# A hybrid decoder kernel: norm steps between the stages emitted one split's length earlier

## The chip, the core and the metric

The kernel runs on one core of a Trainium2 chip. The core has five engines with a queue of instructions each: TensorE (PE) multiplies, VectorE (DVE) and ScalarE (ACT) work elementwise, GpSimd (POOL) does small steps, and SyncE (SP) issues the DMAs. Engines wait for each other by semaphores. The metric is the device time of one execution in microseconds; less is better.

## The reference

Two layers, each a token mixer and a feed-forward network (FFN), both wrapped in RMS norms before and after. All inputs and weights are float32; 256 tokens of width 1024.

```
def rmsnorm(x, g):
    y = xf * lax.rsqrt(jnp.mean(xf * xf, axis=-1, keepdims=True) + RMS_EPS)
    return (y * g.astype(F32)).astype(x.dtype)

def swiglu(h, w_gate, w_up, w_down):
    return (jax.nn.silu(h @ w_gate) * (h @ w_up)) @ w_down

for l in range(DEPTH):
    m = hybrid_mixer(rmsnorm(h, mix_pre_norm[l]), w_in[l], ..., w_out[l])
    h = h + rmsnorm(m, mix_post_norm[l])
    f = swiglu(rmsnorm(h, ffn_pre_norm[l]), w_gate[l], w_up[l], w_down[l])
    h = h + rmsnorm(f, ffn_post_norm[l])
```

The mixer projects to 3088 columns, runs dilated softmax attention (8 heads) beside chunked gated linear attention (4 heads), and projects back with `w_out`. The FFN is 2816 wide.

## The kernel before

The 256 tokens are two row halves of 128, `j` = 0 and 1; each keeps its residual `h[j]` in SBUF. A product must be nearly float32-exact, so each operand is split in two parts of a narrower type: a high part (`wh`, `xh`), which ACT makes by a copy, and a low part (`wl`, `xl`), which DVE makes as operand minus high part. A product is then three matmuls: high by high, low by high, high by low. Weights stream in through four `raw` slots of 128x1024 and are split into eight pairs `wh`/`wl`. One such piece is called a part here: the gate matrix of an FFN chunk (`FF_CHUNKS`) has four parts, the up matrix too, and each serves both row halves. A slot takes its next load when the low half of what was in it has been made.

The FFN's chunks 1, 3 and 4 (`SEVEN`) save one of eight block products by sums of weight blocks (`b11`, `b21`, `v1`, ..., shown as `b` and `v`) and sums of activation blocks (`sums_x`: four `a` sums, split to `sums_h` and `sums_l`).

The order on every engine comes from a planner that runs while the kernel is built (`Clock`). It holds an estimated time for each engine and counts TensorE's as "now". Each piece of work is a generator: `yield t` puts it to sleep until the planner's clock reaches `t`, and then it emits its next instructions. `soon(x)` is the time at which the planner thinks `x` is written. `highs()` and `lows_()` emit the weight splits on ACT and DVE whenever the planner's clock for that engine is no more than `AHEAD` (0.3 and 0.7 us) ahead of now; `loader` emits the loads and `project` the matmuls.

Between the mixer and the FFN, `post_norm` takes the two PSUM banks of `w_out`'s product (`wo`): `square` on ACT (`sq`, `msh`), the gain on DVE (`pn`), `var` on DVE, `rstd` on POOL, and the update of `h` on DVE. `pre_norm_ffn` follows: `sq` on `h`, `var`, `rstd`, the scaled copies `xn` on ACT, TensorE's transposes (`tp_x`), a copy with the gain into `a` (four instructions), `xh_x` on ACT and `xl_x` on DVE; after the second row half come the `a` sums. The FFN of a layer begins with the products `b11` (`seven_a`) and `b21` (`seven_b`) for row half 0, then gate and up of chunk 0 for row half 0, then both for row half 1. ACT loads the table for SiLU in front of its first use, on `p` (the sum of the first two products).

Of the kernel before, what the change touches and what calls it, by code (L numbers as in the profile page):

```python
# [51 lines left out]
UNITS1 = [("gqk", 0), ("aq", 0), ("gqk", 1), ("aq", 1)] + UNITS0[2:]  # L52
BANKS = {"mm": 2, "tp": 2, "ac": 4}
SEM = 0.2


class Engine:
# [50 lines left out]
class Clock:  # L108
# [40 lines left out]
    def note(self, eng, cost, ins, outs):  # L149
# [3 lines left out]
        for ap in ins:  # L153
            r = self.ready(ap)
            start = max(start, r if eng == "PE" and ap in outs else r + SEM)
        if eng == "DMA":
# [21 lines left out]
    def tile(self, pool, shape, dtype, tag, bufs, name):  # L178
# [3 lines left out]
        while len(slots) >= bufs:  # L182
            done = [t for t in slots if t not in self.open]
            if done:
                t = min(done, key=lambda t: self.last.get(t, 0.0))
                slots.remove(t)
                free = self.last.get(t, 0.0) + SEM
                yield free
# [8 lines left out]
    def close(self, *tiles):  # L197
        for t in tiles:
            self.open.discard(t.tensor.name)

    def after(self, new, old):

        self.free[new.tensor.name] = self.last.get(old.tensor.name, 0.0) + SEM

# [33 lines left out]
def trunk(ctx: ExitStack, tc: tile.TileContext, io: dict):  # L238
# [7 lines left out]
    ck = Clock(nc)  # L246
    pe, act, dve, pool, dma, close = ck.pe, ck.act, ck.dve, ck.pool, ck.dma, ck.close

    def at(*aps):
        return ck.ready(*aps) + 0.5  # L250

    def soon(*aps):

        return ck.ready(*aps)

    def bank(tag, name):
        t = yield from ck.tile(ps, [P, 512], F32, tag, BANKS[tag], name)
        ck.port[t.tensor.name] = ("", 0.0)
        return t

    def t2(name):
        return ck.tile(sb, [P, 512], F32, "t2", NT2, name)
# [4 lines left out]
    def small(name, n=1):  # L267
        return sb.tile([P, n], F32, tag="small", bufs=20, name=name)
# [259 lines left out]
    def load_gain(i):  # L528
        if i < len(gains):
            gtiles[i] = gain(gains[i], D, "gain", 1)  # L530


    def rstd_of(parts_, n):

        v = small("var", n)
        if len(parts_) == 1:
            dve.tensor_scalar(v, parts_[0], EPS, None, op0=ALU.add)
        else:
            dve.scalar_tensor_tensor(v, parts_[0], EPS, parts_[1], op0=ALU.add, op1=ALU.add)
        r = small("rstd", n)  # L540
        pool.tensor_tensor(r, v, nhalf[:, :n], op=ALU.pow)
        return r

    def transpose_pe(src, t0, m, tp):
        for i in range(m):
            pe.transpose(tp[:, i * P:(i + 1) * P], src[:, (t0 + i) * P:(t0 + i + 1) * P], ident)
        return tp.rearrange("p (k t) -> p k t", t=P)[:, :m, :]
# [44 lines left out]
    def pre_norm_ffn(j, out, l):  # L592


        ms = []
        for i in range(2):
            c = slice(i * 512, (i + 1) * 512)
            junk = yield from ck.tile(sb, [P, 512], BF16, "t2", NT2, "sq")
            yield soon(h[j][:, c])
            m = small("ms")  # L600
            act.activation(junk, h[j][:, c], AF.Square, scale=1.0 / 32.0, accum_out=m)
            close(junk)
            ms.append(m)
        yield soon(*ms)
        r = rstd_of(ms, 1)
        xs = []
        if j == 0:
            sums_of[l] = []
            for name, dtype in (("a", F32), ("sums_h", R32), ("sums_l", R32)):
                t = yield from ck.tile(sb, [P, 4, 512], dtype, "big", NBIG, name)  # L610
                sums_of[l].append(t)
        while len(sums_of[l]) < 3:
            yield ck.now() + 0.1
        a = sums_of[l][0]
        for i in range(2):
            c = slice(i * 512, (i + 1) * 512)
            x = yield from t2("xn")
            yield soon(r)
            act.activation(x, h[j][:, c], AF.Copy, scale=r)
            xs.append(x)  # L620
        xt = []
        for i in range(2):
            hi = yield from ck.tile(sb, [P, 4, P], R32, f"xt{j}", 6, "xh_x")
            lo = yield from ck.tile(sb, [P, 4, P], R32, f"xt{j}", 6, "xl_x")
            yield at(xs[i])
            tp = yield from bank("tp", "tp_x")
            tv = transpose_pe(xs[i], 0, 4, tp)
            close(xs[i])
            yield soon(tp)
            av = a[:, 2 * j + i, :]  # L630
            for k in range(4):
                g = 16 + 8 * l + 4 * i + k
                act.activation(av[:, k * P:(k + 1) * P], tv[:, k, :], AF.Copy, scale=gcol[:, g:g + 1])
            close(tp)
            yield soon(av)
            act.activation(hi.rearrange("p k t -> p (k t)"), av, AF.Copy)
            yield soon(hi)
            dve.tensor_tensor(lo.rearrange("p k t -> p (k t)"), av,
                              hi.rearrange("p k t -> p (k t)").bitcast(F32), op=ALU.subtract)
            xt += [(hi[:, k, :], lo[:, k, :]) for k in range(4)]  # L640
        out[j] = xt
        if j == 1:
            yield from sums_x(out, l)

    def sums_x(out, l):

        t, hi, lo = sums_of[l]
        yield soon(t)
        dve.tensor_tensor(t[:, 3, :], t[:, 2, :], t[:, 3, :], op=ALU.subtract)
        dve.tensor_tensor(t[:, 2, :], t[:, 0, :], t[:, 2, :], op=ALU.subtract)  # L650
        dve.tensor_tensor(t[:, 0, :], t[:, 3, :], t[:, 0, :], op=ALU.subtract)
        dve.tensor_tensor(t[:, 1, :], t[:, 1, :], t[:, 0, :], op=ALU.add)
        for row, name in ((0, "s2"), (3, "s1"), (2, "s3"), (1, "s4")):
            yield soon(t[:, row, :])
            act.activation(hi[:, row, :], t[:, row, :], AF.Copy)
            yield soon(hi[:, row, :])
            dve.tensor_tensor(lo[:, row, :], t[:, row, :], hi[:, row, :].bitcast(F32),
                              op=ALU.subtract)
            out[2][name] = [(hi[:, row, k * P:(k + 1) * P], lo[:, row, k * P:(k + 1) * P])
                            for k in range(4)]  # L660
        close(t)
        out[2]["tiles"] = (hi, lo)
# [10 lines left out]
    def post_norm(j, banks, gi, then):  # L673

        g = gtiles[gi]
        ms, ts = [], []

        def square(i):
            junk = yield from t2("sq")
            yield soon(banks[i])  # L680
            m = small("msh")
            act.activation(junk, banks[i], AF.Square, scale=1.0 / 32.0, accum_out=m)
            close(junk)
            ms.append(m)

        def gained(i):
            t = yield from t2("pn")
            yield ck.port[banks[i].tensor.name][1]
            dve.tensor_tensor(t, banks[i], g[:, i * 512:(i + 1) * 512], op=ALU.mult)
            close(banks[i])  # L690
            ts.append(t)

        yield from square(0)
        if ck.ready(banks[1]) <= ck.at["Act"]:
            yield from square(1)
            yield from gained(0)
        else:
            yield from gained(0)
            yield from square(1)
        yield soon(*ms)  # L700
        r = rstd_of(ms, 1)
        yield from gained(1)
        yield soon(r)
        for i, w in ((0, 512), (512, 256), (768, 256)) if j and then is None else ((0, 512), (512, 512)):
            c = slice(i, i + w)
            dve.scalar_tensor_tensor(h[j][:, c], ts[i // 512][:, i % 512:i % 512 + w], r, h[j][:, c],
                                     op0=ALU.mult, op1=ALU.add)
            if then is None:
                dma.dma_start(io["out"][0, j * P:(j + 1) * P, c], h[j][:, c])
        close(*ts)  # L710
        if j == 1:
            load_gain(gi + 1)
        if then is not None:
            yield from then


    def mixer(l, xin, xout):
# [482 lines left out]
        for j in range(2):  # L1200
            while mixed[j][4] is None:
                yield ck.now() + 0.2
            bk = []
            for i in range(2):
                o = yield from bank("ac", f"wo{i}")
                bk.append(o)
            for part, lo in (("wo_g", 4), ("wo_a", 0)):
                while mixed[j][lo] is None:
                    yield ck.now() + 0.2
                yield from project((l, part), mixed[j][lo:lo + 4], bk, first=(lo == 4),  # L1210
                                   last=(lo == 0))
                close_x(mixed[j][lo:lo + 4])
            go(post_norm(j, bk, gi, pre_norm_ffn(j, xout, l)))


    def ffn(l, xin, xout):
# [163 lines left out]
        for j in range(2):  # L1380
            yield from down(nch - 2, j)
            yield from down(nch - 1, j)
            then = pre_norm(j, xout, l + 1) if l + 1 < L else None
            ck.spawn(post_norm(j, acc[j], gi, then), ck.now())
# [19 lines left out]
    h = [const.tile([P, D], F32, name=f"h{j}") for j in range(2)]  # L1404
# [110 lines left out]
```

## Time and profile before

| | |
|---|---|
| three runs | 641.35, 641.0, 639.06 us; median 641.0 |
| profiled execution | 639.99 us in all, span 638.2 us |
| TensorE matmul busy | 622.1 us (97%) |
| DVE busy | 504.3 us (79%) |
| ACT busy | 412.6 us (65%) |
| mean granted TensorE clock | 0.989 |
| HBM read | 107.60 MB |

The span runs from the first to the last instruction. Busy time counts instructions that run, not waits; matmuls overlap each other, so a busy TensorE is not TensorE at its peak. In a timeline a row gives start, duration, engine, line, operation, output and inputs, shape and count, and in brackets the idle time before it with what ended it. All instructions bear the line of the recording helper, 77, so they are told apart by names.

### The profile page before, as it was taken

What the parts mean: (1) busy time and instruction counts of PE and PEld (TensorE: products, weight loads), DVE (VectorE), ACT (ScalarE), POOL (GpSimd) and SP (SyncE); (2) the same over time, 40 slices, a digit from 0 to 9 for tenths busy, and PEclk for the clock granted to TensorE, in tenths of its full rate; (3) what the DMA queues carried; (4) which work ended last, traced back from release to release, by engine and by line L of the source; (5) the groups of instructions that cost most, each with busy time, mean ns of one, the idle gap of its engine ahead of it and who ended that gap; (6) DMA issues with size and microseconds to landing.
All of it is one profiled execution on the core that took longest, in us unless ns stands there. A gap on an engine that the chain in (4) does not pass through costs nothing.

```text
span 638.2 us, 10255 instructions
## 1 busy us (share of the span) xinstructions
PE 622.1 (97%) x3896; PEld 510.7 (80%) x3896; DVE 504.3 (79%) x784; ACT 412.6 (65%) x700; POOL 23.7 (4%) x41
## 2 busy tenths in 40 slices
PE   8999999989999999999999999999899999999995
PEld 7987778868888888879788777887788888888894
DVE  4899975579897899987588996557899778989743
ACT  6889855486946385656577797537966555838531
POOL 1000021000000000000010000110000000000000
PEclk9999999979999999999999999999899999999998
DMA  8965455156048946039474714840910895710811
GB/s 281 281 193 156 149 188 191 52 174 255 1 142 294 397 152 201 1 104 289 142 246 149 205 46 126 277 142 17 368 45 3 286 353 216 270 61 1 263 68 66
DMA packets 53108, 109.30 MB, mean 171 GB/s; under 512 B 5890, under 2 KB 10692, under 8 KB 53060
## 3 DMA queue, kind: packets, MB, share of 16 engines
q1 hardware_dynamic: 53060, 108.66, 51.4%
q8 instruction: 30, 0.49, 0.3%
q14 instruction: 18, 0.15, 0.1%
HBM read 107.60 MB, written 1.05 MB: 170 GB/s over the span
## 4 chain that ended last, share of the span: by engine, by line
PE 86%; DVE 5%; DMA 3%; ACT 3%; issue 2%; SPq 1%; POOLq 0%; DVEq 0%; ACTq 0%
PE dn L77 17%; PE seven_a L77 10%; PE gate_ps L77 8%; PE up_ps L77 8%; PE seven_b L77 7%; PE wo L77 4%; PE gr L77 4%; PE gqk L77 4%; PE ak L77 4%; PE gv L77 3%; PE av L77 3%; PE aq L77 3%; DVE wl L77 3%; ACT wh L77 2%; PE att_o L77 2%
## 5 line engine op out<-in xcount | busy, mean ns | idle before, releaser
L77 DVE TENSOR_TENSOR wl<-raw,wh 128x1024 fp32r<-128x1024 f32 (+1 forms) x124 | 150.3, 1221 | 32.4 <-ACT wh L77 31.6
L77 ACT ACTIVATE wh<-raw 128x1024 fp32r<-128x1024 f32 (+1 forms) x124 | 130.0, 1059 | 54.1 <-DMA raw<-w_gate 17.3
L77 ACT ACTIVATE wh<-b 128x1024 fp32r<-128x1024 f32 x72 | 75.0, 1058 | 38.2 <-PE up_ps L77 9.3
L77 DVE TENSOR_TENSOR wl<-b,wh 128x1024 fp32r<-128x1024 f32 x72 | 84.9, 1218 | 2.9 <-ACT wh L77 2.8
L77 PE MATMUL dn<-wh,xh_h 128*128 128x512 f32 x176 | 70.4, 400 | 0.0
L77 PE MATMUL dn<-wl,xh_h 128*128 128x512 f32 x176 | 69.5, 395 | 0.0
L77 PE MATMUL dn<-wh,xl_h 128*128 128x512 f32 x176 | 69.1, 393 | 0.0
L77 DVE TENSOR_TENSOR b<-b,b 128x1024 f32<-128x1024 f32 x36 | 42.7, 1217 | 0.0
L77 POOL TENSOR_TENSOR rstd<-var,nhalf 128x1 f32<-128x1 f32 (+1 forms) x24 | 21.2, 883 | 557.6 <-DVE var L77 557.5
L77 PEld LDWEIGHTS dn<-wl,xh_h 128*128 128x128 f32 x176 | 33.1, 188 | 8.2 <-DVE wl L77 1.4
L77 PEld LDWEIGHTS dn<-wh,xl_h 128*128 128x128 f32 x176 | 33.0, 188 | 7.4
L77 PEld LDWEIGHTS dn<-wh,xh_h 128*128 128x128 f32 x176 | 33.1, 188 | 7.0
L77 DVE SCALAR_TENSOR_TENSOR wl<-raw,gcol,wh 128x512 fp32r<-128x512 f32 (+1 forms) x48 | 34.4, 748 | 1.6 <-ACT wh L77 1.6
L77 ACT ACTIVATE wh<-raw,gcol 128x512 fp32r<-128x512 f32 (+1 forms) x48 | 32.4, 717 | 4.7 <-DMA raw<-w_in 3.3
L77 PE MATMUL gate_ps<-wh,xh_x 128*128 128x512 f32 (+1 forms) x96 | 34.9, 363 | 0.0
L77 PE MATMUL up_ps<-wh,xh_x 128*128 128x512 f32 (+1 forms) x96 | 34.3, 358 | 0.0
L77 PE MATMUL gate_ps<-wh,xl_x 128*128 128x512 f32 (+1 forms) x96 | 34.1, 356 | 0.0
L77 PE MATMUL gate_ps<-wl,xh_x 128*128 128x512 f32 (+1 forms) x96 | 34.1, 355 | 0.0
L77 PE MATMUL up_ps<-wh,xl_x 128*128 128x512 f32 (+1 forms) x96 | 34.1, 355 | 0.0
L77 PE MATMUL up_ps<-wl,xh_x 128*128 128x512 f32 (+1 forms) x96 | 34.1, 355 | 0.0
L77 ACT ACTIVATE xh_h<-tp_h 128x512 fp32r<-128x512 f32 (+1 forms) x24 | 13.3, 554 | 25.1 <-PE tp_h L77 24.9
L77 DVE TENSOR_TENSOR xl_h<-tp_h,xh_h 128x512 fp32r<-128x512 f32 (+1 forms) x24 | 15.5, 645 | 14.9 <-ACT xh_h L77 14.8
(233 smaller groups left out, 1483.9 us busy)
## 6 DMA issues: line engine op xcount, KB each, us to landing
raw<-w_in SPq DMA_DIRECT2D x45, 512.0 KB, 4.6
raw<-w_down SPq DMA_DIRECT2D x44, 512.0 KB, 4.9
b<-w_gate SPq DMA_DIRECT2D x24, 512.0 KB, 8.2
b<-w_up SPq DMA_DIRECT2D x24, 512.0 KB, 7.5
raw<-w_gate SPq DMA_DIRECT2D x20, 512.0 KB, 4.4
raw<-w_up SPq DMA_DIRECT2D x20, 512.0 KB, 4.8
raw<-w_out SPq DMA_DIRECT2D x16, 512.0 KB, 3.7
raw<-w_in SPq DMA_DIRECT2D x6, 256.0 KB, 5.1
```

Source lines behind the costliest of these rows:

```text
L77: return f(*args, **kw)
```

## The change

A constant `LEAD` of 1.1 us and a helper `next_`, which is `soon` less `LEAD`, are added. In `pre_norm_ffn` and `post_norm` the waits of the planner use `next_` in place of `soon`, so these steps are emitted when the planner's clock stands 1.1 us before their inputs; one wait (on `av`) is left out, and one takes `ts` in besides `r`.

```
+LEAD = 1.1
...
+    def next_(*aps):
+
+        return ck.ready(*aps) - LEAD
...
-            yield soon(h[j][:, c])
+            yield next_(h[j][:, c])
             m = small("ms")
             act.activation(junk, h[j][:, c], AF.Square, scale=1.0 / 32.0, accum_out=m)
...
-        yield soon(*ms)
+        yield next_(*ms)
         r = rstd_of(ms, 1)
...
-            yield soon(r)
+            yield next_(r)
             act.activation(x, h[j][:, c], AF.Copy, scale=r)
...
-            yield soon(tp)
+            yield next_(tp)
...
-            yield soon(av)
             act.activation(hi.rearrange("p k t -> p (k t)"), av, AF.Copy)
-            yield soon(hi)
+            yield next_(hi)
...
-            yield soon(banks[i])
+            yield next_(banks[i])
...
-            yield ck.port[banks[i].tensor.name][1]
+            yield ck.port[banks[i].tensor.name][1] - LEAD
...
-        yield soon(*ms)
+        yield next_(*ms)
         r = rstd_of(ms, 1)
         yield from gained(1)
-        yield soon(r)
+        yield next_(r, *ts)
```

The three places below are in layer 0 between the mixer and the FFN; layer 1 has the same order there. `raw_1430`, `raw_1432`, `raw_1451` and `raw_1483` are the four gate parts of chunk 0, `raw_1739` and the next are up parts after the change.

DVE before, around the update of the second row half's `h` (`h1`):

```order
L77 TENSOR_TENSOR wl_1632<-raw_1430,wh_1631 128x1024
L77 TENSOR_TENSOR wl_1647<-raw_1432,wh_1646 128x1024
L77 TENSOR_TENSOR wl_1665<-raw_1451,wh_1664 128x1024
L77 TENSOR_TENSOR pn_1687<-wo0_1561,gain_952 128x512
L77 SCALAR_TENSOR_TENSOR var_1693<-msh_1682,msh_1685 128x1
L77 TENSOR_TENSOR pn_1697<-wo1_1562,gain_952 128x512
L77 TENSOR_TENSOR xl_x_1637<-a_1619,xh_x_1636 128x512
L77 TENSOR_TENSOR wl_1680<-raw_1483,wh_1679 128x1024
L77 SCALAR_TENSOR_TENSOR h1_88<-pn_1687,rstd_1695,h1_88 128x512
```

All four gate parts are split ahead of `h1`. DVE after, from the first gate part on (`h1` stands above, with one split of `b21` and a `var` between):

```order
L78 TENSOR_TENSOR wl_1679<-raw_1430,wh_1678 128x1024
L78 TENSOR_TENSOR wl_1709<-raw_1432,wh_1708 128x1024
L78 TENSOR_TENSOR p1_1715<-seven_b_1717,p1_1715 128x512
L78 TENSOR_TENSOR wl_1738<-raw_1451,wh_1737 128x1024
L78 TENSOR_TENSOR xl_x_1745<-a_1603,xh_x_1744 128x512
L78 TENSOR_TENSOR xl_x_1789<-a_1603,xh_x_1788 128x512
L78 TENSOR_TENSOR a_1603<-a_1603 128x512 x4
L78 TENSOR_TENSOR wl_1765<-raw_1483,wh_1764 128x1024
L78 TENSOR_TENSOR wl_1813<-raw_1739,wh_1812 128x1024
L78 TENSOR_TENSOR sums_l_1605<-a_1603,sums_h_1604 128x512 x4
L78 TENSOR_TENSOR wl_1816<-raw_1753,wh_1815 128x1024
```

All gate parts now come after `h1`; the fourth stands behind both `xl_x` of the second row half and the four `a` sums, and the second up part behind the four `sums_l`.

ACT before, from the third gate part on:

```order
L77 ACTIVATE wh_1664<-raw_1451 128x1024
L77 ACTIVATE sq_1681,msh_1682<-wo0_1561 128x512
L77 ACTIVATE sq_1684,msh_1685<-wo1_1562 128x512
L77 ACTIVATE xh_x_1636<-a_1619 128x512
L77 ACTIVATE wh_1679<-raw_1483 128x1024
L77 ACTIVATE a_1619<-tp_x_1703,gcol_89 128x128 x4
L77 ACTIVATE xh_x_1701<-a_1619 128x512
```

Between the third and the fourth gate part stand two squares and one `xh_x`, the first row half's. ACT after, from the third gate part on:

```order
L78 ACTIVATE wh_1737<-raw_1451 128x1024
L78 ACTIVATE a_1603<-tp_x_1766,gcol_89 128x128 x4
L78 ACTIVATE xh_x_1744<-a_1603 128x512
L78 ACT_TABLE_LOAD
L78 ACTIVATE p1_1715<-p1_1715 128x512
L78 ACTIVATE a_1603<-tp_x_1790,gcol_89 128x128 x4
L78 ACTIVATE xh_x_1788<-a_1603 128x512
L78 ACTIVATE wh_1764<-raw_1483 128x1024
```

The fourth gate part has moved behind the second row half's two sets of copies, the table load and the SiLU.

TensorE's order at this place changes only in where the transposes stand: those of the first row half come after nine and after fifteen of the last 24 matmuls of `wo` (before: after fifteen and after all 24), those of the second one within the gate product for row half 0, behind its first and its second part. In the mixer of layer 1 the order moves on several engines (the transposes of `h`, the `ex` steps of the linear attention, `fine` and `score` products), and SP's loads stay in order but for two small gain loads.

## Rows read from the trace of the kernel before

**Rows 1.** The page: span, and busy time of each engine

```profile
span 638.2 us, 10255 instructions
...
PE 622.1 (97%) x3896; PEld 510.7 (80%) x3896; DVE 504.3 (79%) x784; ACT 412.6 (65%) x700; POOL 23.7 (4%) x41
```

**Rows 2.** Stretches: us, busy PE, PEld, DVE, ACT, POOL, clock, DMA share, GB/s

```profile
133.50:137.00 3.50, 1.10 (x5) 0.37 (x3) 3.02 (x6) 3.50 (x10) 0.55 (x1) 0.89 0.90 290
137.00:143.00 6.00, 5.88 (x14) 4.62 (x15) 4.36 (x6) 4.10 (x11) 0.00 (x0) 0.50 0.88 247
...
329.00:334.00 5.00, 4.66 (x27) 3.64 (x26) 2.71 (x7) 2.49 (x11) 0.00 (x0) 1.00 1.04 403
334.00:430.00 96.00, 95.99 (x926) 78.12 (x925) 72.95 (x187) 65.55 (x143) 4.99 (x8) 1.00 0.51 159
468.00:630.00 162.00, 162.00 (x772) 133.87 (x771) 131.08 (x135) 92.06 (x110) 0.55 (x1) 1.00 0.44 153
```

**Rows 3.** Timeline of TensorE, layer 0, from the seam to the mark

```profile
133.22 0.60 PE L77 MATMUL tp_x<-ident,xn 128*128 128x128 f32 x4
...
135.66 0.50 PE L77 MATMUL seven_a<-wh,xh_x 128*128 128x512 f32 x1 [1.85 <-ACT xh_x L77]
...
137.12 0.80 PE L77 MATMUL seven_a<-wh,xl_x 128*128 128x512 f32 x1 [0.67 <-DVE xl_x L77]
...
151.01 0.39 PE L77 MATMUL up_ps<-wh,xh_x 128*128 128x512 f32 x1
151.24 0.40 PE L77 MATMUL up_ps<-wl,xh_x 128*128 128x512 f32 x1
...
156.99 0.40 PE L77 MATMUL gate_ps<-wh,xh_x 128*128 128x512 f32 x1
```

**Rows 4.** Timeline of TensorE, layer 1, the same two places

```profile
445.32 0.60 PE L77 MATMUL tp_x<-ident,xn 128*128 128x128 f32 x4
...
467.92 0.40 PE L77 MATMUL gate_ps<-wh,xh_x 128*128 128x512 f32 x1
```

**Rows 5.** Timeline of ACT, layer 0, at the seam

```profile
121.27 0.60 ACT L77 ACTIVATE sq<-wo 128x512 f32<-128x512 f32 x1 [2.26 <-PE wo L77]
...
133.83 0.59 ACT L77 ACTIVATE sq<-wo 128x512 f32<-128x512 f32 x1
...
142.29 0.62 ACT L77 ACTIVATE sq<-h 128x512 bf16<-128x512 f32 x1
...
142.90 2.00 ACT L77 ACTIVATE wh<-raw 128x1024 fp32r<-128x1024 f32 x2
...
147.09 1.28 ACT L77 ACT_TABLE_LOAD   x1
148.38 0.63 ACT L77 ACTIVATE p<-p 128x512 f32<-128x512 f32 x1
148.92 1.12 ACT L77 ACTIVATE a<-tp_x,gcol 128x128 f32<-128x128 f32 x4
```

**Rows 6.** Timeline of DVE, layer 0, at the seam

```profile
123.57 1.42 DVE L77 SCALAR_TENSOR_TENSOR h<-pn,rstd,h 128x512 f32<-128x512 f32 x2
...
131.07 2.36 DVE L77 TENSOR_TENSOR wl<-raw,wh 128x1024 fp32r<-128x1024 f32 x2 [0.76 <-ACT wh L77]
...
136.99 1.22 DVE L77 TENSOR_TENSOR wl<-raw,wh 128x1024 fp32r<-128x1024 f32 x1
...
143.03 0.16 DVE L77 SCALAR_TENSOR_TENSOR var<-ms 128x1 f32<-128x1 f32 x1 [1.48 <-ACT sq L77]
...
156.22 2.87 DVE L77 TENSOR_TENSOR a<-a 128x512 f32<-128x512 f32 x4
...
165.87 1.29 DVE L77 TENSOR_TENSOR sums_l<-a,sums_h 128x512 fp32r<-128x512 f32 x2
```

**Rows 7.** Timeline of POOL, layer 0

```profile
127.41 0.55 POOL L77 TENSOR_TENSOR rstd<-var,nhalf 128x1 f32<-128x1 f32 x1 [3.87 <-DVE var L77]
```

**Rows 8.** The page's DMA issues: count, KB each, us from issue to landing

```profile
raw<-w_up SPq DMA_DIRECT2D x20, 512.0 KB, 4.8
```

## The prediction

> **What bounds the kernel now.** I read the page first: the span is 638.2 us and TensorE is busy 97% of it [rows 1]. So a change in order gains only where TensorE waits or runs at its low clock, and it loses wherever it makes TensorE wait. Next I read the table of stretches around the seams between stages [rows 2]. At the seam from the mixer to the FFN in layer 0 (133.5 to 137.0 us) TensorE works 1.10 of 3.50 us. From 137.0 to 143.0 us the granted clock is 0.50, the 1.2 GHz level: 14 matmuls take 5.88 us, 0.42 each. TensorE's timeline [rows 3] names the causes: 1.85 us until ACT has written `xh_x`, then 0.67 us until DVE has written `xl_x`. It idled there, and the clock fell. At full clock matmuls start 0.23 us apart, and a gate or up product of eight steps (24 matmuls) with one block of transposes takes 5.98 us (151.01 to 156.99). In layer 1 the same seam stands 312.10 us later [rows 4]. The seam from the FFN to the next mixer has almost no idle time: 0.34 us in 329 to 334, and 95.99 of 96.00 us are busy up to 430 [rows 2].
>
> I therefore read the time at one mark: the first matmul of the second row half's gate product, at 156.99 in layer 0 and 467.92 in layer 1 [rows 3, 4]. Behind it TensorE is never short of work (162.00 of 162.00 us in layer 1 [rows 2]), so a delay at the mark is a delay of the end.
>
> **The change part by part.** The diff adds no operation. It puts the norm's steps up to 1.1 us earlier into the queues of ACT and DVE, so weight splits fall behind them. A split takes ACT 1.06 us (0.95 until the next starts) and DVE 1.22 us (1.14 until the next) [rows 5, 6]. Each queue runs in the order of emission. I lay out the new order of layer 0 step by step: an instruction starts when its engine is free and its input is written.
>
> First row half: `h` is written from 123.57 as before. The two `sq` steps stand behind one split instead of two, at 124.35 and 125.03. `var` follows its `sq` by 0.74 at least (142.29 to 143.03) [rows 5, 6]; DVE is in a split until 126.05. `var` with its hand-over takes some 0.25 us and `rstd` 0.55 [rows 6, 7], so `xn` starts at 126.9. The transposes stand earlier in TensorE's queue, at 129.3 and 131.05. A block takes 0.60 us, the four scaled copies `a` 1.12, and `xh_x` comes behind them [rows 3, 5]: 131.1 and 132.9, with `xl_x` at 131.8 and 133.5. TensorE is through with `wo` and both blocks at about 133.55 (the last of them started at 133.22 and idleness began at 133.81) and goes on without a pause: **both waits of the seam, 1.85 and 0.67 us, go**.
>
> What is late next? Four splits that were done by 138.2 (the fourth gate part's low half started at 136.99) [rows 6] now stand behind the norm of the second row half.
> - The last split of `b21` reaches ACT at 133.4. The second half's `sq` on `wo` starts at 134.35 (was 133.83), and `h` comes 2.30 us after it, as 121.27 to 123.57 shows [rows 5, 6]: 136.65 to 138.0. Only then DVE splits `b21`: done 139.2. TensorE reaches that part at 137.95: **1.3 us wait**.
> - `sq` on `h` at 137.4 and 138.1, `var` 139.1, `xn` 139.95. The first three gate parts have their low halves at 140.4, 141.55 and 143.5, and TensorE is through with them and both blocks of transposes at 145.4.
> - The fourth gate part has both halves behind the whole path of the second row half. On ACT: `a` 142.4, `xh_x` 143.6, the table load 144.2 (1.28 us), the SiLU on `p` 145.5, `a` 146.05, `xh_x` 147.2, and then the split at 147.7, done 148.8. On DVE: `xl_x` 147.85, the four sums `a` at 148.6, which take 2.87 us, and then the split, 151.4 to 152.6 [rows 5, 6]. TensorE stands from 145.4 to 152.6 but for one matmul: **7.0 us wait**.
> - The up parts: DVE does one split (done 153.75), four `sums_l` (0.61 apart [rows 6]) to 156.1, then three splits, done 157.35, 158.45 and 159.6. The fourth part's load needs the slot that the fourth gate part frees at 152.6 and lands 4.8 us later [rows 8], in time for its place. TensorE ends the gate product at 153.8 and the first up part at 155.2, waits 1.9 us for the second, and is through at 161.3 at full clock.
>
> The clock: waits of 2.5 us in all came before the low level in rows 2 and 3, so I expect it behind the 7 us too, and charge the row's price, 0.42 us a matmul, for as long a stretch as there. The first up part then ends at 157.35, just when the second is ready, so only the tail is dearer: 162.2. I take 161.7, between the row and none. The mark comes 4.7 us later than 156.99 (bounds 4.3 and 5.2). In layer 1 the same steps end at 161.7 + 312.1 = 473.8 against 467.92, 5.9 us later (5.4 and 6.4); before, that seam had lost less.
>
> Behind the mark the sums and splits of the seven products keep a margin: by the same reckoning their low halves are 0.5 to 2.9 us ahead of TensorE, so nothing is added. The mixer of layer 1 is reshuffled too (transposes, `ex`, `fine`, `score`). Its splits run several us ahead, and I take 0, with bounds from the nearest rows: -0.34 (its only idle time goes) and +0.67 (one wait behind a DVE operation, as at 137.12) [rows 2, 3].
>
> On ACT's table load a rule of the Trainium skill speaks against the forecast. The rows [rows 5] show 1.28 us, and the SiLU starts at 148.38, 0.01 us behind it. The page "ScalarE: Activation LUTs", section "What ACT_TABLE_LOAD costs", gives about 2.66 us for a switch, a drain of about 1.38 us being counted beside the load. By the page the two layers would be some 2.8 us dearer, since the load now stands on the path; by the row nothing is added. I go by the row.
>
> **Sum.** 4.7 + 5.9 + 0 = +10.6 us. Span 638.2 + 10.6 = 648.8; the profiled execution took 639.99 in all, so 650.6. The median of the runs, 641.0, lies 1.0 above that execution, and the forecast for a median is 641.0 + 10.6, or **651**. Its own range is 647 to 656: the bounds above, and some 2 us a layer for the rounding of twenty hand-overs between engines.
>
> **The rivals.**
> - **Faster: the seam closes and no split is late.** One mechanism: the fourth gate part's low half is written before TensorE wants it (145.6). Then the mark of layer 0 comes at 133.55 + 24 x 0.23 + 2 x 5.98 = 151.0, 6.0 us earlier, and that of layer 1 4.8 earlier: 641.0 - 10.8 = 630. For it speaks that the waits of the seam do go; against it that DVE's queue has two `xl_x` and four sums in front of that split. The point from which it decides is 148: a split done by then, 4.6 us before my 152.6, offsets the loss. 6 in 100.
> - **Even.** The path of the second row half runs some 4 us quicker than laid out, so that the stall pays back just what the seam gives: 638 to 644. 8 in 100.
> - **Dearer behind the mark.** The margin of 0.5 us at the sums is eaten and DVE falls a split or two (1.14 us each) behind in each layer: 653 to 657. 9 in 100.
> - **The table load holds ACT longer.** It now stands between the two `xh_x` of the second half. If ACT stood as long again as the load itself, 1.28 us in each layer, the time would be 651 + 2.6 = 654. No row shows such a pause: 3 in 100. It is the rule of the page named above.
> - **The diff does nothing at the seam.** Excluded by the order of the built kernel: the splits do stand behind.
>
> **How the numbers follow.** The forecast has 74 in 100. A measurement of this kernel can tell about 0.5%, 3.2 us, from no change. Faster takes the first rival and a little of the second, 0.07; within 0.5% the rest of the second, 0.08 with a little of the forecast's low end; slower has 0.85. The range for 8 in 10 takes in the forecast's own and the dearer cases, down to 645: 645 to 657.
>
> **What would show it.** In the profile after, TensorE starts `seven_a` without a wait near 133.5 (first step right). ACT's second `xh_x` and DVE's four sums `a` of the second row half run at 147 to 151.5 instead of up to 159. TensorE's longest wait is a gate matmul on DVE's `wl`, about 3.5 us, behind one on ACT's `wh` of about 3.4 us, in each layer. Its waits at the two seams, 5 us before, come to about 20. The low clock stands somewhere in 146 to 158. The marks stand near 161.7 and 478.5. I am wrong if that wait is under 3 us, or if TensorE makes the loss good behind the mark.

## The result and the profile after

The changed kernel takes 655.7 us (median of four runs, 655.20 to 659.38) against 640.6 us for the kernel before, measured beside it. The ratio is 1.0251, with a 95% interval from 1.0209 to 1.0293, so it is slower by about 15 us. The forecast was 651, about 10 us slower, its range 645 to 657.

The page of the profiled execution (655.66 us) answers [rows 1]:

```profile
span 653.9 us, 10243 instructions
...
PE 625.4 (96%) x3896; PEld 511.0 (78%) x3896; DVE 504.0 (77%) x784; ACT 413.3 (63%) x700; POOL 26.0 (4%) x41
```

The span is 15.7 us longer. DVE and ACT are busy as long as before; TensorE is busy 3.3 us more, since it ran more often at its low clock, and GpSimd 2.3 us more, of which more is said below. Five stretches of the kernel after, with the columns of [rows 2]:

```profile
134.00:137.00 3.00, 3.00 (x15) 2.44 (x14) 1.81 (x4) 3.00 (x7) 0.22 (x1) 1.00 0.00 0
147.50:155.10 7.60, 1.02 (x2) 0.29 (x1) 4.62 (x7) 7.56 (x14) 0.00 (x0) 0.74 0.20 65
155.10:158.00 2.90, 2.88 (x7) 2.30 (x8) 2.90 (x5) 1.41 (x4) 0.00 (x0) 0.50 0.59 163
400.00:404.00 4.00, 4.00 (x16) 3.37 (x16) 1.01 (x3) 2.62 (x10) 0.00 (x0) 0.57 0.06 20
485.00:645.00 160.00, 160.00 (x762) 132.05 (x761) 129.77 (x130) 89.92 (x106) 0.55 (x1) 1.00 0.48 162
```

The first row is the old seam, now full. The hole has moved to 147.5 to 155.1 us: two matmuls in 7.60 us, and the 1.2 GHz level behind it. The fourth row is a low clock in the mixer of layer 1 that was not there before. The last row answers the last one of [rows 2]: behind the mark of layer 1 TensorE is never idle.

TensorE's timeline at the seam of layer 0, and the mark of layer 1, answer [rows 3, 4]:

```profile
134.39 0.39 PE L78 MATMUL seven_a<-wh,xh_x 128*128 128x512 f32 x1
...
139.97 0.50 PE L78 MATMUL seven_b<-wl,xh_x 128*128 128x512 f32 x1 [1.05 <-DVE wl L78]
...
143.47 0.66 PE L78 MATMUL tp_x<-ident,xn 128*128 128x128 f32 x4 [0.70 <-ACT xn L78]
...
151.31 0.79 PE L78 MATMUL gate_ps<-wh,xh_x 128*128 128x512 f32 x1 [3.58 <-ACT wh L78]
155.12 0.80 PE L78 MATMUL gate_ps<-wl,xh_x 128*128 128x512 f32 x1 [3.02 <-DVE wl L78]
...
159.80 0.50 PE L78 MATMUL up_ps<-wl,xh_x 128*128 128x512 f32 x1 [0.33 <-DVE wl L78]
...
163.84 0.40 PE L78 MATMUL gate_ps<-wh,xh_x 128*128 128x512 f32 x1
...
483.28 0.39 PE L78 MATMUL gate_ps<-wh,xh_x 128*128 128x512 f32 x1
```

`seven_a` starts without a wait, the last split of `b21` comes 1.05 us late, and the fourth gate part costs 3.58 us on its high and 3.02 us on its low half. The marks are 6.85 and 15.36 us later than in [rows 3, 4].

To see where time goes stage by stage, I read seven points from each TensorE timeline: the first `gqk` matmul (an early product of the mixer) and the first `wo` matmul in each layer, the two marks, and the last matmul. All stages in us, the other kernels as the difference from the kernel before (a plus is a loss):

| kernel | L0 mixer | L0 `wo` to mark | mark to L1 `gqk` | L1 mixer | L1 `wo` to mark | mark to end |
|---|---|---|---|---|---|---|
| before | 84.39 | 52.30 | 165.50 | 95.76 | 49.67 | 163.16 |
| after | +0.90 | +6.09 | -0.87 | +2.11 | +7.27 | +0.27 |
| row0 | 0.00 | +3.23 | +1.99 | +1.57 | +5.02 | +0.80 |
| post_only | +1.73 | -0.44 | -0.61 | +0.53 | +1.86 | +0.27 |
| pre_only | +0.01 | +5.04 | -1.23 | -0.08 | +6.23 | -0.05 |
| mix_seam | +3.67 | +6.03 | -0.57 | -0.03 | +7.23 | +0.21 |
| row0_hold | +1.61 | -3.27 | +5.35 | -0.02 | -2.42 | +4.78 |
| after_hold | +1.99 | +4.05 | +3.40 | +0.54 | +3.41 | +4.27 |
| rstd_clear | +0.02 | +5.17 | -0.27 | +0.64 | +6.24 | +0.24 |
| table_early | +3.18 | +5.07 | -0.34 | +0.50 | +6.27 | +0.20 |
| hold_cut | +1.65 | -3.93 | +4.63 | +3.04 | -2.62 | +3.82 |
| copies0_05 | +3.28 | -4.08 | +2.85 | -0.06 | -3.32 | +4.03 |
| copies0_05_table | +3.24 | -3.03 | +4.02 | +1.51 | -3.22 | +4.04 |
| tp0_03 | +1.82 | -1.57 | +3.42 | -0.07 | -0.26 | +4.12 |

The first column is a warning. No edit touches the order of that stage, and yet it varies by 3.7 us among the profiled executions. Nearly all of that is TensorE's clock: the nine kernels that lost 1.6 us or more there show a stretch at the 1.2 GHz level between 93 and 101 us, and the five that lost 0.9 or less show none. The stretch of the kernel before, then that of mix_seam, with the columns of [rows 2]:

```profile
93.00:100.00 7.00, 7.00 (x47) 6.03 (x47) 2.31 (x7) 5.03 (x17) 0.00 (x0) 1.00 0.96 358
```

```profile
93.00:100.00 7.00, 7.00 (x26) 5.30 (x27) 0.67 (x4) 3.74 (x13) 0.00 (x0) 0.51 0.94 335
```

The totals of the runs scatter with the clock too: of the 29 runs of the kernel before that stood beside copies0_05, the eight with a mean granted clock of 0.989 average 640.1 us, the ten with 0.986 average 642.6. So the seam columns, where kernels of the same order agree within 0.1 us (after and mix_seam), tell small edits apart, and the total of one execution doesn't.

### The profile page after: what moved, and what is told of

It is laid out like the page before. It is cut to its first block, busy times and chain, and to the rows that moved or that the text cites. A ratio compares the mean times of both kernels' runs of the same rounds, so it can differ in the third digit from the quotient of the medians.

```text
span 653.9 us, 10243 instructions
## 1 busy us (share of the span) xinstructions
PE 625.4 (96%) x3896; PEld 511.0 (78%) x3896; DVE 504.0 (77%) x784; ACT 413.3 (63%) x700; POOL 26.0 (4%) x41
## 3 DMA queue, kind: packets, MB, share of 16 engines
HBM read 107.60 MB, written 1.05 MB: 166 GB/s over the span
## 4 chain that ended last, share of the span: by engine, by line
PE 86%; ACT 5%; DVE 3%; DMA 2%; issue 1%; POOL 1%; SPq 1%; POOLq 0%; DVEq 0%; ACTq 0%
PE dn L78 19%; PE seven_a L78 9%; PE up_ps L78 8%; PE gate_ps L78 7%; PE seven_b L78 7%; PE wo L78 6%; PE gr L78 4%; PE ak L78 4%; PE gv L78 4%; PE av L78 3%; PE gqk L78 2%; DMA raw<-w_in 2%; PE aq L78 2%; PE att_o L78 2%; PE coarse L78 2%; PE tp_h L78 1%
## 5 line engine op out<-in xcount | busy, mean ns | idle before, releaser
L78 POOL TENSOR_TENSOR rstd<-var,nhalf 128x1 f32<-128x1 f32 (+1 forms) x24 | 23.5, 977 | 580.2 <-DVE var L78 580.0
L78 PE MATMUL gate_ps<-wl,xh_x 128*128 128x512 f32 (+1 forms) x96 | 35.6, 371 | 6.6 <-DVE wl L78 6.4
L78 DVE TENSOR_TENSOR xl_h<-tp_h,xh_h 128x512 fp32r<-128x512 f32 (+1 forms) x24 | 15.5, 645 | 15.1 <-ACT xh_h L78 15.1
```

The source lines that it names most:

```text
L78: return f(*args, **kw)
```

## The experiments

**Only the first row half early (row0), and only one of the two functions early (post_only, pre_only).** The theory to test was A: the loss comes from the second row half's steps, which stand ahead of the gate splits.

```
+    def near(j, *aps):
+        return soon(*aps) if j else next_(*aps)
...
-            yield next_(h[j][:, c])
+            yield near(j, h[j][:, c])
```

and so at every `next_` of both functions. In post_only and pre_only one function is the changed one and the other is as before.

> The early emission is kept for the first row half only; the second row half's norm steps are emitted when their inputs are ready, as before. Theory A (the loss comes from the second row half's steps standing ahead of the gate splits): in the built order all four gate parts are split on DVE ahead of the second row half's xl_x, so the fourth gate part is on time, the waits of 3.0 to 3.6 us on its wh and wl go, the seam's 1.85 and 0.67 us stay away, and the time is 630 to 638 us. Rival B (the first row half's early steps delay the splits by themselves): the waits in front of the gate product stay above 3 us a layer and the time is 647 us or more.

row0 took 653.81 us, ratio 1.0181 (1.0133 to 1.0229): theory A fell with its 630 to 638 us. Its first half was true: TensorE no longer waits more than 0.4 us in the gate product. But the wait only moved on. DVE and TensorE of row0, layer 0:

```profile
151.02 0.68 DVE L78 TENSOR_TENSOR xl_x<-a,xh_x 128x512 fp32r<-128x512 f32 x1
151.63 2.41 DVE L78 TENSOR_TENSOR v<-b,b 128x1024 f32<-128x1024 f32 x2
153.96 0.68 DVE L78 TENSOR_TENSOR xl_x<-a,xh_x 128x512 fp32r<-128x512 f32 x1
154.68 2.87 DVE L78 TENSOR_TENSOR a<-a 128x512 f32<-128x512 f32 x4
157.46 1.22 DVE L78 TENSOR_TENSOR wl<-raw,wh 128x1024 fp32r<-128x1024 f32 x1
```

```profile
158.73 0.80 PE L78 MATMUL up_ps<-wl,xh_x 128*128 128x512 f32 x1 [5.91 <-DVE wl L78]
```

The last up part's split now stands behind the `v` sums, two `xl_x` and the `a` sums, and TensorE waits 5.91 us for it. Rival B had the time (647 us or more), but not the cause: the first half's early steps did not hold the gate splits.

> Early emission in post_norm only, pre_norm_ffn as before. By theory A the squares, transposes and xl_x of the second row half stand where they stood, behind the gate splits, so the fourth gate part is on time; the seam's wait for the first row half stays, and is longer by up to 1.4 us since the second half's update of h now stands ahead of xl_x: 641 to 645 us. If the update of h ahead of the gate splits were what delays them, the time would be 650 us or more.

645.95 us, ratio 1.0083 (1.0059 to 1.0107), 1 us above what theory A gave; the seam lost nothing in layer 0 and 1.86 us in layer 1.

> Early emission in pre_norm_ffn only, post_norm as before. The seam's waits for the first row half go (about -2.5 us and the low clock behind it). The second half's update of h comes later than in the changed kernel, so three gate parts are split ahead of its xl_x and the fourth one's high half stands behind its rstd and xn: by theory A a shorter wait at the fourth gate part, 0 to 3 us a layer, and 634 to 644 us. If early squares and copies alone made the whole loss: 652 us or more.

652.32 us, ratio 1.0179 (1.0139 to 1.0218): a miss, 8 us above theory A's upper end and at the rival's 652. The stage table agrees: `pre_norm_ffn` alone costs 5.04 and 6.23 us at the seams, nearly all that the whole change costs there. Its waits lie at the up parts, 2.12 us on `wh` and 2.54 us on `wl` in layer 0.

**The other seam as before (mix_seam).** In `post_norm` of the FFN, `next_` is `soon` again:

```
-            yield next_(banks[i])
+            yield near(gi % 2, banks[i])
```

> As the changed kernel at the seam from mixer to FFN, as before at the seam from FFN to mixer. It asks where the 2.15 us that the mixer of layer 1 lost come from. Theory: from the reordering that the early steps at the FFN's end cause (a low clock at 400 us of the changed kernel's span although TensorE is busy): that stretch runs at full clock and the time is 653 to 654 us. Rival: the mixer is reordered by the lateness carried from layer 0: the low clock stays and the time is 655 to 656 us.

The mixer of layer 1 takes 95.73 us, as before (95.76), instead of 97.87, at full clock throughout. The row of mix_seam, with the columns of [rows 2]:

```profile
330.00:426.00 96.00, 95.66 (x932) 78.10 (x932) 76.17 (x193) 70.78 (x158) 6.10 (x9) 1.00 0.55 171
```

The total did not follow: 655.96 us, ratio 1.0224 (1.0188 to 1.0261), which is the rival's figure, but with an interval of some 2.3 us to either side it can't tell 2 us; in the profiled execution the 2.1 us were hidden by a first stage 2.8 us longer than in the profile of after, at the low clock shown above. Nor does the theory stand as a whole. The later kernels of the table split the 2.11 us in two. Some 0.5 us comes with early steps at the FFN's end for both row halves: post_only, after_hold, rstd_clear and table_early lost 0.50 to 0.64 us there at full clock, and the kernels without such steps nothing. The other 1.5 us is the low clock, and it isn't tied to these steps: copies0_05_table, which has none, has it and lost 1.51 us (hold_cut, 3.04 us, and row0 likewise), while copies0_05 with the same order on TensorE ran at full clock. The stretches of the two, copies0_05_table first:

```profile
395.00:410.00 15.00, 15.00 (x66) 12.26 (x66) 8.05 (x10) 11.90 (x25) 1.02 (x1) 0.92 0.32 93
```

```profile
395.00:410.00 15.00, 15.00 (x81) 12.79 (x80) 9.99 (x12) 11.29 (x30) 1.02 (x1) 1.00 0.54 169
```

The eighth column is the granted clock, 0.92 against 1.00. Among the fourteen profiled executions, one for each kernel, it fell in this mixer in four; how often it does so in one kernel was not measured.

**The sums held back (row0_hold, after_hold).** Theory C: what counts is whatever stands ahead of the last of the eight gate and up splits on DVE. The `a` sums, and the first `v` sums likewise, wait for those splits:

```
+        while lows[0] <= where[l, "up", 0][-1]:
+            yield ck.now() + 0.1
         yield soon(t)
         dve.tensor_tensor(t[:, 3, :], t[:, 2, :], t[:, 3, :], op=ALU.subtract)
```

> row0 with one more rule: the four a sums and the first v sums wait until DVE has all four up parts' low splits in its queue. Theory C (the loss comes from whatever stands ahead of the last of the eight gate and up splits on DVE; in row0 that was the last up part, behind two v sums, an xl_x and four a sums, 5.9 us): the last up part's split starts near 151.6 us in layer 0 instead of 157.46, the wait of 5.9 us and the low clock behind it go in both layers, and the time is 634 to 642 us. Rival D (the sums are only moved, and the seven products stall on them later): a wait of 3 us or more on wh or wl of v or b appears behind 165 us, and the time is 647 us or more.

645.77 us, ratio 1.0074 (1.0053 to 1.0095). The seams gained 3.27 and 2.42 us against the kernel before, as theory C says, and the stretches behind the marks lost 5.35 and 4.78 us, as rival D says, though in several waits under 2 us and not in the one of 3 us that it named. The time lies between the two, above theory C's 642 and below rival D's 647. Two stretches of row0_hold behind the mark:

```profile
164.00:172.00 8.00, 6.18 (x29) 4.57 (x28) 8.00 (x9) 5.24 (x6) 0.00 (x0) 1.00 0.00 0
172.00:180.00 8.00, 7.38 (x32) 5.58 (x31) 8.00 (x8) 5.07 (x7) 0.00 (x0) 1.00 0.00 0
```

And the same place in the kernel before:

```profile
157.00:173.00 16.00, 16.00 (x75) 13.10 (x74) 14.42 (x17) 13.40 (x18) 0.00 (x0) 1.00 0.00 1
```

Before, TensorE is full there and DVE has 1.6 us to spare. In row0_hold DVE is full (16.00 of 16.00) and TensorE is short by 2.4 us: it reaches the seven products sooner than DVE can make their sums and splits.

> The changed kernel with the same rule for the a and v sums. Theory C: in the fourth gate part the wait on wl falls from 3.0 to 3.3 us to about 0.9 us, since its split no longer stands behind the four a sums of 2.87 us; the wait of 3.6 us on wh stays, because nothing moves on ACT ahead of that split; 650 to 652 us. Rival D: the sums are late for the seven products instead, 654 us or more.

The wait on `wl` fell as theory C said. TensorE of after_hold:

```profile
152.04 0.80 PE L78 MATMUL gate_ps<-wh,xh_x 128*128 128x512 f32 x1 [3.58 <-ACT wh L78]
153.30 0.80 PE L78 MATMUL gate_ps<-wl,xh_x 128*128 128x512 f32 x1 [0.47 <-DVE wl L78]
```

From 3.02 to 0.47 us, with 3.58 us on `wh` unmoved. So the four `a` sums in front of that split are what the second wait of the changed kernel consists of. The time was 656.87 us, ratio 1.0262 (1.0225 to 1.0299), as rival D had it: the seams lost 2.0 and 3.9 us less than in the changed kernel, and the stretches behind the marks 4.3 and 4.0 us more.

**Less work for DVE (hold_cut).**

```
-        dve.tensor_tensor(t[:, 3, :], t[:, 2, :], t[:, 3, :], op=ALU.subtract)
+        dve.eng.tensor_tensor(t[:, 3, 0:64], t[:, 2, 0:64], t[:, 3, 0:64], op=ALU.subtract)
```

and so for all four sums: seven eighths of each are left out, so this part of the FFN is not computed.

> row0_hold with the four a sums done on 64 of their 512 columns (the rest of the sums is left out, so this part of the FFN is not computed), in the same order. That takes 2.87 us of DVE work per layer down to about 0.5 us. Theory E (behind the mark DVE, busy 8.00 of 8.00 us there in row0_hold, is the bound; what the seam gains is paid back because DVE has a fixed amount of work up to the seven products): from the mark to the end of each FFN falls by about 2.3 us a layer, and the time from 645.8 to 640 to 642.5 us. Rival F (TensorE's waits there come from the order of transposes and copies, not from the amount of DVE's work): the waits behind the mark stay, 645 to 647 us.

644.77 us, ratio 1.0043 (1.0018 to 1.0067): above theory E's range and just under rival F's. The kernels before that stood beside the two differ as well (640.86 us for row0_hold, 641.97 for hold_cut); against them the loss fell from 4.9 to 2.8 us. The stretches behind the marks fell by 0.72 and 0.96 us, though DVE was spared some 1.9 us a layer (the four sums take 0.92 us, not 2.87). In layer 1 row0_hold also ran at the low clock for a while (0.83 granted from 480 to 490 us) and hold_cut didn't, so the first number is the cleaner one. So the amount of DVE's work is part of the bound there, by about half at most; the rest stays with the order in which DVE and TensorE wait for each other there, which these runs don't take apart.

**GpSimd's rstd by itself (rstd_clear).** A 128x1 instruction on DVE reads the second half's `rstd`; all else is in place:

```
         r = rstd_of(ms, 1)
+        if j:
+            dve.eng.tensor_scalar(small("seen"), r, 1.0, None, op0=ALU.mult)
```

> The changed kernel with one small DVE instruction per layer (128x1, it reads the second row half's rstd) between var and the two gate splits; all else stands in the same order. It keeps DVE from running splits while GpSimd computes rstd. Theory (GpSimd's rstd of 2.54 and 2.60 us was held by DVE's two splits, whose inputs both lie in SBUF): rstd takes 0.55 us in both layers, xn starts about 2.0 us earlier, the splits 1.0 us later; the wait for wh in the fourth gate part shrinks by about 1 us a layer: 652.5 to 654.5 us. Rival (rstd is slow for a reason of its own, as its place or its inputs): it still takes over 2 us, and the time is 656 to 658 us.

GpSimd's and DVE's timelines of rstd_clear:

```profile
138.94 0.55 POOL L78 TENSOR_TENSOR rstd<-var,nhalf 128x1 f32<-128x1 f32 x1 [2.80 <-DVE var L78]
...
456.46 0.55 POOL L78 TENSOR_TENSOR rstd<-var,nhalf 128x1 f32<-128x1 f32 x1 [2.74 <-DVE var L78]
```

```profile
139.52 0.15 DVE L612 TENSOR_SCALAR seen<-rstd 128x1 f32<-128x1 f32 x1 [0.73 <-POOL rstd L78]
139.60 2.36 DVE L78 TENSOR_TENSOR wl<-raw,wh 128x1024 fp32r<-128x1024 f32 x2
...
148.24 0.69 DVE L78 TENSOR_TENSOR xl_x<-a,xh_x 128x512 fp32r<-128x512 f32 x1 [2.94 <-ACT xh_x L78]
```

0.55 us in both layers instead of 2.54 and 2.60: DVE's splits had held it. The seams came 0.92 and 1.03 us sooner than in the changed kernel, the 1 us forecast. That is the gain less what the small instruction costs: it holds DVE for 0.73 us, and TensorE then waits for one of the splits behind it:

```profile
140.88 0.50 PE L78 MATMUL gate_ps<-wl,xh_x 128*128 128x512 f32 x1 [0.46 <-DVE wl L78]
```

The time was 654.19 us (651.48 to 655.65), ratio 1.0216 (1.0181 to 1.0250).

**The table load by itself (table_early).**

```
         g = gtiles[gi]
+        if gi % 2 == 0 and j == 0:
+            act.eng.preload_act_table(AF.Silu)
```

> The changed kernel with ACT's table load in front of the first row half's square of wo, where ACT idles 2.25 us, instead of in front of the SiLU; all else stands in the same order. Theory (the load lies on the path in the changed kernel and costs its own 1.28 us and no more): the second row half's copies and the fourth gate part's split come 1.28 us earlier, the waits in the gate product shrink by about 1.3 us a layer: 652.5 to 654 us. Rival (the switch holds ACT for some 2.66 us): 649.5 to 651.5 us. Rival (the load is covered by a wait for tp_x): 655 to 656.5 us.

TensorE of table_early:

```profile
152.40 0.50 PE L78 MATMUL gate_ps<-wh,xh_x 128*128 128x512 f32 x1 [2.15 <-ACT wh L78]
```

The seams came 1.02 and 1.00 us sooner than in the changed kernel, and the wait on `wh` fell from 3.58 to 2.15 us. So the load lay on the path, and moving it saved 1.0 us of its 1.28. By the Trainium skill, "ScalarE: Activation LUTs", section "What ACT_TABLE_LOAD costs", a switch takes about 2.66 us; an estimate from that figure is a gain of up to 2.66 us a layer from moving it away, and the stages show 1.0. The total, 655.22 us with runs from 650.55 to 658.64, ratio 1.0219 (1.0165 to 1.0274), can't tell the theories apart.

**Smaller doses (copies0_05, copies0_05_table, tp0_03).** The kernel before, with only the first half's last steps early:

```
-            yield soon(tp)
+            yield near(j, tp)
...
-            yield soon(av)
+            if j:
+                yield soon(av)
...
-            yield soon(hi)
+            yield near(j, hi)
```

with `LEAD` 0.5; tp0_03 leaves the last of the three out and has 0.3.

> The kernel before with one small part of the change: only the first row half's last steps (the four scaled copies, xh_x, xl_x) are emitted ahead, by 0.5 us instead of 1.1; squares, rstd, xn, post_norm and the second row half as before. Theory E (what counts is DVE's idle time between the first update of h and the splits of the seven products, 6.5 us in the kernel before, 12.5 us in the changed one): the wait of 1.85 us on xh_x falls under 0.5 us, DVE's idle time stays within 1 us of the 6.5 us, and the time is 636 to 640 us. Rival (any step put ahead costs DVE more idle time than TensorE gains): DVE's idle time is 8 us or more and the time is 642 us or more.

643.79 us, ratio 1.0036 (1.0010 to 1.0061): the rival's time, although DVE's idle time, added up from its timeline, is the theory's (6 to 7 us a layer). So theory E, in the form that it has here, had the wrong measure. Both waits of the seam went and the seams gained 4.08 and 3.32 us, the most of all; behind the marks 2.85 and 4.03 us were paid back. TensorE's waits in copies0_05:

```profile
PE tp_h L78 <- DVE sg L78: 2.1, 2, 1.1
PE up_ps L78 <- DVE wl L78: 2.0, 4, 0.7
...
PE seven_b L78 <- DVE wl L78: 1.2, 2, 0.6
...
PE seven_a L78 <- DVE wl L78: 0.9, 4, 0.2
```

These four, at the seams and behind the marks, name DVE, and it is full again where the payback lies:

```profile
166.00:182.00 16.00, 14.08 (x60) 10.29 (x58) 16.00 (x16) 11.73 (x14) 0.00 (x0) 1.00 0.00 0
```

> copies0_05 with ACT's table load in front of the first row half's square of wo, where ACT idles. The load of 1.28 us leaves the stretch in which ACT makes the up parts' high halves. Theory: those come 1.28 us earlier where ACT is the one waited for, DVE idles less, and the time is 0.5 to 2 us under copies0_05. Rival (ACT has slack there): the same time as copies0_05 within 0.5 us.

643.84 us, ratio 1.0032 (1.0008 to 1.0055): the same, and the seam and the stretch behind it, taken together, lost more than in copies0_05 and not less. So the rival holds and ACT has slack there; the interval would still hide a gain of 0.5 us.

> The kernel before with a still smaller part: only the first row half's scaled copies are emitted 0.3 us ahead and xh_x right behind them; xl_x as before. The first xh_x stands ahead of one split and of both squares of the second half's wo, the second one still behind the squares. Theory E: the wait of 1.85 us on xh_x goes, part of it comes back at xl_x or the second block (up to 1 us), and the time is 637 to 641 us. Rival: DVE's idle time grows by 2 us or more and the time is 642 us or more.

648.35 us, ratio 1.0101 (1.0060 to 1.0143), the rival's side. The seams gained 1.57 and 0.26 us and the stretches behind lost 3.42 and 4.12 us, there with a wait of 1.8 us for a split and the low clock behind it. No version beat the kernel before.

## Why the prediction was right, and which terms were off

The direction, the places and the two engines were right. Of the forecast's steps, each measured from the first `wo` matmul (which came 0.76 us later in the profile of after, with no part of the change ahead of it):

- **Both seam waits go**: yes, in both layers.
- **1.3 us at `b21`'s last split**: 1.05 and 0.92 us.
- **7.0 us at the fourth gate part, 3.4 on `wh` and 3.55 on `wl`**: 3.58 and 3.02 us in layer 0, 3.58 and 3.33 us in layer 1. The sizes held, but the place came 1.5 us later than laid out, for the reason below.
- **1.9 us at the second up part at full clock, none behind the low one**: 0.33 us. TensorE was slowed by the low clock and met a split that was nearly done.
- **The mark of layer 0, +4.7 us**: +6.09. **That of layer 1, +5.9 us**: +7.27. Both lie above their bounds (5.2 and 6.4). This is the mis-sized term. The step that failed is "`var` with its hand-over takes some 0.25 us and `rstd` 0.55", taken for the second row half too. GpSimd, DVE and ACT of the kernel after:

```profile
127.01 0.55 POOL L78 TENSOR_TENSOR rstd<-var,nhalf 128x1 f32<-128x1 f32 x1 [2.73 <-DVE var L78]
136.78 0.55 POOL L78 TENSOR_TENSOR rstd<-var,nhalf 128x1 f32<-128x1 f32 x1 [9.21 <-DVE var L78]
140.13 2.54 POOL L78 TENSOR_TENSOR rstd<-var,nhalf 128x1 f32<-128x1 f32 x1 [2.80 <-DVE var L78]
```

```profile
139.83 0.15 DVE L78 SCALAR_TENSOR_TENSOR var<-ms 128x1 f32<-128x1 f32 x1
139.90 2.36 DVE L78 TENSOR_TENSOR wl<-raw,wh 128x1024 fp32r<-128x1024 f32 x2
...
145.01 1.23 DVE L78 TENSOR_TENSOR wl<-raw,wh 128x1024 fp32r<-128x1024 f32 x1 [2.16 <-ACT wh L78]
...
150.34 0.69 DVE L78 TENSOR_TENSOR xl_x<-a,xh_x 128x512 fp32r<-128x512 f32 x1 [2.94 <-ACT xh_x L78]
151.06 2.87 DVE L78 TENSOR_TENSOR a<-a 128x512 f32<-128x512 f32 x4
153.85 2.35 DVE L78 TENSOR_TENSOR wl<-raw,wh 128x1024 fp32r<-128x1024 f32 x2
```

```profile
142.70 1.33 ACT L78 ACTIVATE xn<-h,rstd 128x512 f32<-128x512 f32 x2 [2.15 <-POOL rstd L78]
...
146.69 1.28 ACT L78 ACT_TABLE_LOAD   x1
147.99 0.63 ACT L78 ACTIVATE p<-p 128x512 f32<-128x512 f32 x1
...
149.68 0.63 ACT L78 ACTIVATE xh_x<-a 128x512 fp32r<-128x512 f32 x1
```

`rstd` stretches over both splits that run beside it, ACT waits 2.15 us for it, and DVE then waits 2.16 us for a `wh` that ACT makes behind it. (The 2.94 us for the second `xh_x` have another cause: they stand in rstd_clear too, behind the table load and the SiLU.) Less the 0.76 us of the late start, `var` ran as laid out (139.07 for 139.1), `xn` 2.0 us late (141.94 for 139.95), and the table load, the second `xh_x` and the fourth gate part's split on DVE 1.7 us late each (153.09 for 151.4). From that split to the mark it took 0.3 us less than laid out, which leaves the 1.4 us. rstd_clear shows 0.92 and 1.03 us of them by experiment, net of what its own instruction costs; that the rest has the same cause is read from these rows and was not tested by itself. The kernel before showed the price already, at the seam from the FFN to the mixer, in rows that I had not looked at:

```profile
322.82 2.35 DVE L77 TENSOR_TENSOR wl<-raw,wh 128x1024 fp32r<-128x1024 f32 x2
```

```profile
323.04 2.53 POOL L77 TENSOR_TENSOR rstd<-var,nhalf 128x1 f32<-128x1 f32 x1 [7.98 <-DVE var L77]
```

- **The mixer of layer 1, 0**: +2.11, outside its bounds of -0.34 and +0.67. Those were bounds on waits, and they hold the 0.5 us that the early steps cost; the rest was a low clock without a wait.
- **Behind the marks, 0**: -0.87 (one wait of 1.0 us for `sg` went) and +0.27.

The forecast's 10.6, and 1.4 + 1.4 + 2.1 - 0.9 + 0.3 for these terms and 0.8 for the start, make the 15.7 us of the two spans. (641.0 + 10.6 is 651.6, which the forecast put down as 651.) The table load was charged at its row's 1.28 us, and that held: the SiLU starts 0.02 us behind it.

So the mechanism was right, but the size was short by 4.5 us (15.1 against 10.6), and the forecast's own range of 647 to 656 held by 0.3 us. That is in part luck: the range had 2 us a layer for rounding, and what filled them was no rounding but a held `rstd` and a low clock in the mixer of layer 1, which fell there in only four of the fourteen profiled executions.

What the prediction saw too narrowly is why milder forms of the change did not pay either. It took the seam's 5 us as open to be gained if only the fourth gate part came in time. In every variant that closed the seam or narrowed its wait (row0, pre_only, row0_hold, after_hold and the three small doses) the time came back further on: at the fourth gate part, at the last up part, or at the seven products, where DVE is full. hold_cut shows that DVE's amount of work there is part of the bound; that the rest is order and not something else is argued, not shown.

## What to carry to other kernels

Emitting a step ahead of its input in an in-order queue turns waiting beside other work into idling in front of it; here no dose of it paid, with DVE full at the next point where everything must be ready. Follow a moved queue to the last piece that TensorE needs from it, not to the first, and judge a gain at a seam by the stretch behind it. When a stage that no edit touches varies by more than the effect, look at its granted clock, and compare stages between fixed points of the timelines.

## What the runs showed of the hardware that was not expected

A GpSimd operation on 128x1 elements takes 0.55 us beside an idle DVE and 2.5 us beside two DVE splits of 128x1024, ending 0.4 us behind them; a DVE instruction that waits for it brings it back to 0.55 us. Both inputs of the splits lie in SBUF. Beside `pn`, which reads PSUM, the `rstd` at 136.78 us of the kernel after took 0.55 us. The Trainium skill, "GPSIMD Engine Reference", section "Key points", says that GpSimd shares its SBUF interfaces with DVE and contends with DVE instructions that have two SBUF inputs; the rows agree, and give the price.

TensorE's clock fell to the 1.2 GHz level at about 400.4 us of the kernel after while the profile shows it busy without a gap: ahead of the fall stood 32 `coarse` products of 64 rows and eight transposes, and the `gv` matmuls behind them took 0.43 us each instead of 0.23. In rstd_clear, with TensorE's products in the same order, the clock didn't fall. The mixer of layer 0 shows the same more often: with one order of instructions in all fourteen kernels, the clock fell there in nine profiled executions, at 93.0 to 95.0 us, among or right behind the small `fine` and `coarse` products, and it cost 1.6 to 3.7 us. What decides, these runs don't settle.
